# Retention turned in token halves through other buffers, stores on ScalarE's queue, dense weights fetched ahead

## The chip, the cores and the metric

The kernel runs on one core of a Trainium2 chip. The metric is the device time of one execution in microseconds (us). The core's engines are TensorE (PE: matmuls and transposes), VectorE (DVE), ScalarE (ACT), GpSimd (POOL) and SyncE (SP), which here issues every DMA. Each engine works through its own instructions in order.

## The reference

One block of 1024 tokens and 1024 channels, all in float32: differential attention beside chunkwise retention, merged by gates, then an MLP and a gated embedding.

```python
h = rms_norm(x, g_mix[i]);  proj = h @ w_in[i]
qa, ka, va, qr, kr, vr, gr, gate_a, gate_r = jnp.split(proj, split_idx, axis=-1)
# differential attention, 8 heads: softmax(q1 k1) - lam * softmax(q2 k2), times v, with ALiBi
# retention, 4 heads, chunks of 128, decay g per head:
def step(R, inp):
    qi, ki, vi = inp
    s = jnp.einsum('bnhk,bmhk->bhnm', qi, ki) * decay_intra
    intra = jnp.einsum('bhnm,bmhv->bnhv', s, vi)
    cross = jnp.einsum('bnhk,bhkv->bnhv', qi, R) * q_decay[None, :, :, None]
    R_new = R * chunk_decay[None, :, None, None] + jnp.einsum('bmhk,bmhv,hm->bhkv', ki, vi, k_decay)
    return R_new, intra + cross
yr = jax.nn.silu(gr) * rms_norm(retention(qr, kr, vr), g_ret_sub[i]).reshape(B, S, RET_V_W)
mixed = (jax.nn.sigmoid(gate_a) * (ya @ w_branch_diff[i]) + jax.nn.sigmoid(gate_r) * (yr @ w_branch_ret[i]))
x = x + mixed @ w_out[i];  x = x + square(relu(rms_norm(x, g_mlp[i]) @ w_ff1[i])) @ w_ff2[i]
x = x + sigmoid(rms_norm(x, g_ple[i]) @ w_ple_gate[i]) * (p[i] @ w_ple[i])
return rms_norm(x, g_final)
```

## The kernel before

TensorE multiplies float32 as pairs: `split` (L119 to L122) makes a high half by a cast on ACT (L121) and the rest by a subtraction on DVE (L122), and each product is three matmuls (hi hi, lo hi, hi lo). The stages follow one another: the in-projection to about 508 us; retention, four heads, to about 647 us; attention, eight heads, to about 1043 us; then the merge, the MLP and the rest.

**Dense steps as filler.** The gates' projections and later the branches' are written as generators in `queue`; one step is six 128x512 matmuls (L185 to L187), four steps fill a bank, sixteen do a unit of 256 columns for two token halves. `fill(n)` (L212) puts n steps between the pieces of retention (`RET_FILL`) and attention (`PLAN`). `cols_steps` loads and splits a unit's weights in its first step. A finished bank ("mm", two of them) is drained by `gate_out` (L444: activation L446, store of `gt_d` L447) or, in attention, by `fin_r`: the gate comes back by a load (L985), DVE multiplies it in (L989), and the product is stored (L990).

**Retention.** For each head `ret_qk` loads q and k (L701, 1 MB), multiplies the decays in (L705) and splits; `ret_sg` loads the silu gate (L733, 1 MB) into the slots S2 and S6 by turns; `ret_kn` transposes k (L721); `ret_scores` computes the masked scores in 24 matmuls (L749), writes them to the slot S8 (L751) and splits them to S7; `ret_chain` runs over eight chunks: the state's update (L766) goes to the back of S8 (L769, L771) and is split into `Gb`; the chunk's output is matmuls of S7 and `Gb` (L784), copied to S9 (L787 squares, L788 copies); after the last chunk POOL makes one power of 128x8 and DVE scales all chunks (L792). `ret_turn` turns the head over, for each of two channel blocks e and both token halves: four transposes (L802), the gate (L805, into "o" or "sq"), the split (high half to `Gb`), and two stores to `yr_d` (L88). 

**What sets the order.** A list scheduler puts each engine's instructions in a fixed order when the program is built. DMAs are tracked by eight semaphores by turns, so that each also waits for the one eight before it. A slot that is written again waits for every reader of its old content, stores included.

## Time and profile before

| | us |
|---|---|
| median of 3 runs | 1954.53 (1953.75 to 1958.95) |
| the profiled execution | 1956.08 |
| its span | 1954.1 |
| PE busy | 1898.3 (97%) |
| DVE busy | 1316.5 (67%) |
| ACT busy | 873.2 (45%) |

The span is the profiled execution without what lies around it (2.0 us). Matmuls overlap in the records, so that a dense 128x512 matmul is listed at 0.39 us while the next begins 0.23 us behind it; busy time says only where PE was not idle. The chain of waits gives PE 76% of the span, DVE 10% and DMA 6%.

### The profile page before, as it was taken

What the parts mean: (1) busy time and instruction counts of PE and PEld (TensorE: products, weight loads), DVE (VectorE), ACT (ScalarE), POOL (GpSimd) and SP (SyncE); (2) the same over time, 40 slices, a digit from 0 to 9 for tenths busy, and PEclk for the clock granted to TensorE, in tenths of its full rate; (3) what the DMA queues carried; (4) which work ended last, traced back from release to release, by engine and by line L of the source; (5) the groups of instructions that cost most, each with busy time, mean ns of one, the idle gap of its engine ahead of it and who ended that gap; (6) DMA issues with size and microseconds to landing.
All of it is one profiled execution on the core that took longest, in us unless ns stands there. A gap on an engine that the chain in (4) does not pass through costs nothing.

```text
span 1954.1 us, 24125 instructions
## 1 busy us (share of the span) xinstructions
PE 1898.3 (97%) x8976; PEld 1568.2 (80%) x8976; DVE 1316.5 (67%) x2047; ACT 873.2 (45%) x1370; POOL 108.5 (6%) x120
## 2 busy tenths in 40 slices
PE   8999999999999999999999998999999999999998
PEld 6888788888878778877788887788888888888886
DVE  5877765544667588888897436876766676776633
ACT  6533443334534477766675223433333443344522
POOL 1200000000000111111110002000000000000000
PEclk9999999999999999999999999999999999999999
DMA  8554554532777855876546323444546986555202
GB/s 276 180 173 164 174 179 164 180 120 98 270 256 223 219 155 137 253 221 180 161 154 197 124 76 97 140 148 149 164 132 206 374 313 226 196 183 186 94 11 76
DMA packets 238325, 343.36 MB, mean 176 GB/s; under 512 B 15104, under 2 KB 128896, under 8 KB 236928
## 3 DMA queue, kind: packets, MB, share of 16 engines
q1 hardware_dynamic: 238208, 341.83, 54.0%
q8 instruction: 70, 1.15, 0.2%
q14 instruction: 47, 0.39, 0.1%
HBM read 235.35 MB, written 106.43 MB: 175 GB/s over the span
## 4 chain that ended last, share of the span: by engine, by line
PE 76%; DVE 10%; DMA 6%; issue 4%; ACT 3%; POOL 2%; SPq 0%; POOLq 0%; DVEq 0%; ACTq 0%
PE mm L302 17%; PE qk L302 13%; PE qk L1279 6%; PE mm L187 4%; PE mm L185 4%; PE mm L186 4%; PE sm L1279 3%; PE mm L1279 3%; PE qk L853 2%; PE po L1279 2%; PE po L895 2%; PE qk L310 2%; DMA S<-in_w_in 2%; PE mm L199 1%; PE mm L200 1%
## 5 line engine op out<-in xcount | busy, mean ns | idle before, releaser
L185 PE MATMUL mm<-T,wh 128*128 128x512 f32 x352 | 140.2, 399 | 0.0
L186 PE MATMUL mm<-T,wh 128*128 128x512 f32 x352 | 139.9, 397 | 0.0
L187 PE MATMUL mm<-T,wl 128*128 128x512 f32 x352 | 139.3, 396 | 0.0
L860 ACT ACTIVATE S<-S,stat 128x256 f32<-128x256 f32 (+7 forms) x128 | 98.9, 775 | 37.3 <-DVE stat L855 36.9
L121 ACT CAST wh<-S 128x1024 fp32r<-128x1024 f32 (+1 forms) x60 | 69.2, 1167 | 94.0 <-issue 33.6
L853 PE MATMUL qk<-S,S 128*128 128x512 f32 (+3 forms) x384 | 103.2, 366 | 4.1 <-DVE stat L855 3.9
L229 POOL TENSOR_TENSOR stat<-stat,mhalf 128x1 f32<-128x1 f32 (+1 forms) x28 | 22.7, 809 | 1352.2 <-DVE stat L227 1352.2
L302 PE MATMUL mm<-S,T 128*128 128x512 f32 x384 | 94.3, 395 | 2.6 <-DVE S L122 1.9
L302 PE MATMUL mm<-T,raw 128*128 128x512 f32 x384 | 92.4, 389 | 2.9 <-DVE s L314 2.9
L302 PE MATMUL mm<-S,wh 128*128 128x512 f32 x384 | 93.1, 391 | 0.0
L302 PE MATMUL qk<-S,wh 128*128 128x512 f32 x384 | 92.2, 389 | 0.0
L302 PEld LDWEIGHTS mm<-S,T 128*128 128x128 f32 x384 | 73.0, 191 | 19.1 <-DVE S L122 2.3
L302 PEld LDWEIGHTS mm<-T,raw 128*128 128x128 f32 x384 | 72.0, 188 | 18.3 <-DVE s L314 3.3
L122 DVE TENSOR_TENSOR T<-T,T 128x1024 fp32r<-128x1024 f32 (+2 forms) x28 | 40.3, 1449 | 66.2 <-ACT T L121 66.2
L302 PEld LDWEIGHTS mm<-S,wh 128*128 128x128 f32 x384 | 72.5, 189 | 15.0
L302 PEld LDWEIGHTS qk<-S,wh 128*128 128x128 f32 x384 | 72.1, 188 | 15.0
L855 DVE CUSTOM_DVE_ANT_0 S<-qk,Gb 128x512 f32<-128x512 f32 (+3 forms) x128 | 72.6, 582 | 9.2 <-DMA Gb<-in_alibi 7.7
L121 ACT CAST S<-sm 128x512 fp32r<-128x512 f32 (+2 forms) x116 | 54.5, 493 | 49.4 <-PE sm L880 30.6
L853 PEld LDWEIGHTS qk<-S,S 128*128 128x128 f32 x384 | 62.6, 192 | 16.9 <-DVE stat L855 11.5
L187 PEld LDWEIGHTS mm<-T,wl 128*128 128x128 f32 x352 | 66.6, 189 | 11.7
L185 PEld LDWEIGHTS mm<-T,wh 128*128 128x128 f32 x352 | 66.7, 190 | 11.2
L186 PEld LDWEIGHTS mm<-T,wh 128*128 128x128 f32 x352 | 66.5, 189 | 11.0
(361 smaller groups left out, 4791.8 us busy)
## 6 DMA issues: line engine op xcount, KB each, us to landing
S<-in_w_in SPq DMA_DIRECT2D x52, 512.0 KB, 5.1
S<-qk_d SPq DMA_DIRECT2D x96, 256.0 KB, 5.8
S<-in_w_ff SPq DMA_DIRECT2D x40, 512.0 KB, 5.8
qk_d<-T SPq DMA_DIRECT2D x32, 512.0 KB, 5.1
...
```

Of the source, the lines that this page charges most:

```text
L121: nc.scalar.copy(out=hi, in_=src)
L122: nc.vector.tensor_tensor(out=lo, in0=src, in1=hi.bitcast(F32), op=ALU.subtract)
L185: nc.tensor.matmul(out=ps, lhsT=wh(kt), rhs=ah, start=(kt == 0), stop=False)
L186: nc.tensor.matmul(out=ps, lhsT=wh(kt), rhs=al, start=False, stop=False)
L187: nc.tensor.matmul(out=ps, lhsT=wl(kt), rhs=ah, start=False, stop=(kt == KT - 1))
L302: nc.tensor.matmul(out=ps, lhsT=x[:, k, :], rhs=y[:, k, :], start=(first and k == 0 and n == 0), stop=(k == 3 and n == 2), skip_group_chec ...
L310: nc.tensor.matmul(out=ps, lhsT=x[:, k, cs], rhs=y[:, k, :], start=(first and k == 0 and n == 0), stop=(k == 3 and n == 2), skip_group_che ...
L853: nc.tensor.matmul(out=ps, lhsT=qs[:, c, qsl], rhs=kk[:, c, k0:k0 + kw], start=(m == 0), stop=(m == 1))
L855: nc.vector.tensor_tensor_reduce(out=pr[:, c, k0:k0 + kw], in0=ps, in1=bias[0][:, S - w + k0:S - w + k0 + kw], scale=-1.0, scalar=mx[:, 2 ...
L860: nc.scalar.activation(out=pc, in_=pc, func=AF.Exp, scale=-1.0, bias=mx[:, 2 * c + n:2 * c + n + 1], accum_out=z[:, c:c + 1])
L895: nc.tensor.matmul(out=out, lhsT=v[:, k, :], rhs=a[:, k, q0:256], start=(k == 0 and n == 0), stop=(k == nkt - 1 and n == 2))
L1279: nc.tensor.matmul(out=ps, lhsT=a[x][:, m, k, st * P:(st + 1) * P], rhs=b[y][:, m, k, :], start=(g == 0 and k == 0 and n == 0), stop=(g == ...
```

## The change

- `gate_out`'s store goes on ScalarE's queue, and so do the stores of the high halves in `ret_turn`: 48 issues leave SP for ACT.
- `ret_turn` works on one token half at a time, both channel blocks in it, with three dense steps between the halves. Half 0 has its high halves in the front of S8 and f in "o" and "sq"; half 1 has its high halves in `Gb` and f in the back of S8.
- The power and the scaling of chunks 0 to 3 come after chunk 4, those of 4 to 7 at the end.
- The next head's decays stand after chunks 2 and 5, kept in program order.
- A class `Work` holds a dense unit: the next unit's weights are fetched when six steps of the present one are left and split when three are left. (The merge's first unit gets its weights by the same class.)

```diff
-    def move(out, in_):
-        nc.sync.dma_start(out=out.bitcast(F32), in_=in_.bitcast(F32))
+    def move(out, in_, eng=None):
+        (eng or nc.sync).dma_start(out=out.bitcast(F32), in_=in_.bitcast(F32))
...
+    def fetch_cols(w, c0):
+        raws = []
+        for k0 in (0, 4):
+            raws.append(raw_tile())
+            nc.sync.dma_start(out=raws[-1].rearrange("p (a n) -> p a n", n=256), in_=w_block(w, c0, 256, k0, k0 + 4))
+        return raws
+    def split_cols(raws):
+        hi, lo = slot("wh", F32R, bufs=2), slot("wl", F32R, bufs=2)
+        for i, raw in enumerate(raws):
+            split(raw, hi[:, i * 1024:(i + 1) * 1024], lo[:, i * 1024:(i + 1) * 1024])
+        return [a.rearrange("p (kt n) -> p kt n", n=256) for a in (hi, lo)]
...
+    class Work:
+        def __init__(self, steps, total, w=None, c0=0):
+            self.steps, self.left, self.w, self.c0 = steps, total, w, c0
+            self.raws = self.ops = None
+        def ready(self, to_split=True):
+            if self.w is None:
+                return
+            if self.raws is None:
+                self.raws = fetch_cols(self.w, self.c0)
+            if to_split and self.ops is None:
+                self.ops = split_cols(self.raws)
...
     def fill(n):
         while n > 0 and queue:
+            work = queue[0]
+            work.ready()
             try:
-                next(queue[0])
-                n -= 1
+                next(work.steps)
             except StopIteration:
                 queue.pop(0)
+                continue
+            n -= 1
+            work.left -= 1
+            if len(queue) > 1 and work.left in (6, 3):
+                queue[1].ready(work.left == 3)
...
-        nc.sync.dma_start(out=gt_d[:, unit, hs(half)], in_=o)
+        nc.scalar.dma_start(out=gt_d[:, unit, hs(half)], in_=o)
...
+        def decay(a):
+            x = tmp[:, a].rearrange("p (c n) -> p c n", n=P)
+            tc.keep_in_program_order(nc.vector.tensor_tensor(
+                out=x, in0=x, in1=rtab[h // 2][:, h % 2, a, :][:, None, :].broadcast_to([P, ST, P]), op=ALU.mult))
+        def parts(a):
             d = slot(("S0", "S1")[a], F32R).rearrange("p (a s) -> p a s", a=2)
             for half in range(2):
                 split(tmp[:, a, hs(half)], d[:, 0, hs(half)], d[:, 1, hs(half)])
...
+        decay(1)
+        kd = parts(1)
+        yield
+        decay(0)
+        yield
+        yield parts(0), kd
...
+        def norm(half):
+            four = slice(half * 4, half * 4 + 4)
+            r = rstd_of(ss[:, four], DV)
+            for c in range(half * 4, half * 4 + 4):
+                nc.vector.tensor_scalar(out=yn[:, c, :], in0=yn[:, c, :], scalar1=r[:, c % 4:c % 4 + 1],
+                                        scalar2=None, op0=ALU.mult)
...
-            fill(RET_FILL[0])
-        r = rstd_of(ss, DV)
-        for c in range(ST):
-            nc.vector.tensor_scalar(out=yn[:, c, :], in0=yn[:, c, :], scalar1=r[:, c:c + 1], scalar2=None, op0=ALU.mult)
+            fill_gates(RET_FILL[0])
+            if c == 4:
+                norm(0)
+            if c in (2, 5):
+                next(beside)
+        norm(1)
         return yn
-    def ret_turn(h, yn, sg):
+    def ret_turn(h, yn, sg, s8, half):
+        his = s8[:, 0:S] if half == 0 else slot("Gb", F32, (P, 1024))
         for e in range(2):
-            his = slot("Gb", F32R, (P, 1024)).rearrange("p (a s) -> p a s", a=2)
-            for half in range(2):
-                pt = bank("sm")
...
-                f = slot(("o", "sq")[half], F32, (P, HALF))
...
+            f = s8[:, S + e * HALF:S + (e + 1) * HALF] if half else slot(("o", "sq")[e], F32, (P, HALF))
...
+            hi = his[:, hs(e)].bitcast(F32R)
+            split(f, hi, f.bitcast(F32R))
+            move(yr_d[:, 0, h * 2 + e, hs(half)], hi, nc.scalar)
+            move(yr_d[:, 1, h * 2 + e, hs(half)], f.bitcast(F32R))
...
-        fill(RET_FILL[1])
-        ret_turn(h, yn, sg)
-    drain()
+        fill_gates(1)
+        ret_turn(h, yn, sg, s8, 0)
+        fill_gates(3)
+        ret_turn(h, yn, sg, s8, 1)
+    fill_gates(1 << 30)
```

`branch_work`, `last_gate` and `diff_half` are the old generators put into `Work`. Three places show what moves.

SP, at the change from head 0 to head 1; the loads are head 2's q and k and head 1's gate. Before:

```order
L88 DMA yr_d_72<-Gb_513_4005 128x512 [waits DMAHW7_49,Activation_49]
L88 DMA yr_d_72<-o_515_4011 128x512 [waits DMAHW0_49,DVE_49]
L701 DMA S2_522_4045<-qr_d_70 128x2048 [waits DMAHW1_49,DVE_49]
L88 DMA yr_d_72<-Gb_513_4005 128x512 [waits DMAHW2_49,Activation_49]
L88 DMA yr_d_72<-sq_517_4022 128x512 [waits DMAHW3_49,DVE_49]
L733 DMA S6_523_4047<-sg_d_71 128x2048 [waits DMAHW4_49,PE_49]
```

Now:

```order
L88 DMA yr_d_72<-o_511_3973 128x512 [waits DMAHW0_49,DVE_49]
L88 DMA yr_d_72<-sq_513_3984 128x512 [waits DMAHW2_49,DVE_49]
L149 DMA raw_638_4875<-in_w_in 128x4x256 [waits DMAHW4_49,DMAHW1_49,Activation_49]
L88 DMA yr_d_72<-S8_477_3714 128x512 [waits DMAHW6_49,DVE_49]
L736 DMA S2_525_4056<-qr_d_70 128x2048 [waits DMAHW7_49]
L88 DMA yr_d_72<-S8_477_3714 128x512 [waits DMAHW1_49,DVE_49]
L775 DMA S6_526_4058<-sg_d_71 128x2048 [waits DMAHW2_49,DMAHW3_49,PE_49,Activation_49]
```

Both f stores of half 1 now leave from S8; the second stands behind the 1 MB load.

DVE, at the change from head 1 to head 2, up to the write of the scores (L751 before, L793 now). Before:

```order
L122 TENSOR_TENSOR o_565_4351<-o_565_4351,Gb_563_4345 128x512 [waits Activation_49]
L805 SCALAR_TENSOR_TENSOR sq_567_4362<-sm_566_4357,gret_83,S6_523_4047 128x512 [waits DMAHW6_49,PE_49]
L122 TENSOR_TENSOR S3_568_4368<-sm_569_4369,S3_568_4368 128x512 [waits Activation_49]
L122 TENSOR_TENSOR sq_567_4362<-sq_567_4362,Gb_563_4345 128x512 [waits Activation_49]
L122 TENSOR_TENSOR S3_568_4368<-sm_570_4376,S3_568_4368 128x512 [waits Activation_49]
L751 TENSOR_TENSOR S8_574_4388<-sm_575_4389,s2_521_4043 128x512 [waits PE_49]
L122 TENSOR_TENSOR S7_573_4387<-S8_574_4388,S7_573_4387 128x512 [waits Activation_49]
L705 TENSOR_TENSOR S6_571_4383<-S6_571_4383,s2_521_4043 128x1024 [waits DMAHW2_49]
L751 TENSOR_TENSOR S8_574_4388<-sm_576_4405,s2_521_4043 128x512 [waits PE_49]
```

Now:

```order
L855 SCALAR_TENSOR_TENSOR S8_528_4061<-sm_566_4354,gret_83,S6_526_4058 128x512 [waits PE_49]
L122 TENSOR_TENSOR sq_560_4321<-sq_560_4321,S8_528_4061 128x512 [waits Activation_49]
L855 SCALAR_TENSOR_TENSOR S8_528_4061<-sm_567_4364,gret_83,S6_526_4058 128x512 [waits PE_49]
L122 TENSOR_TENSOR S8_528_4061<-S8_528_4061,Gb_565_4353 128x512 [waits Activation_49]
L122 TENSOR_TENSOR S3_568_4374<-sm_569_4375,S3_568_4374 128x512 [waits Activation_49]
L122 TENSOR_TENSOR S8_528_4061<-S8_528_4061,Gb_565_4353 128x512 [waits Activation_49]
L122 TENSOR_TENSOR S3_568_4374<-sm_570_4382,S3_568_4374 128x512 [waits Activation_49]
L740 TENSOR_TENSOR S6_571_4389<-S6_571_4389,s2_524_4054 128x1024 [waits DMAHW0_49]
L793 TENSOR_TENSOR S8_574_4394<-sm_575_4395,s2_524_4054 128x512 [waits DMAHW2_49,DMAHW3_49,DMAHW1_49,DMAHW4_49,DVE_49,PE_49]
```

The write of the scores now comes behind the decay (L740) and waits for four DMA semaphores beside PE.

PE in attention, at a branch unit of `w_branch_ret` (L185 to L187 before, L196 to L198 now). Before:

```order
L186 MATMUL mm_1135_7203<-T7_1087_6998,wh_1088_7003 128x512
L187 MATMUL mm_1135_7203<-T6_1086_6997,wl_1089_7004 128x512
L185 MATMUL mm_1135_7203<-T6_1086_6997,wh_1088_7003 128x512
L186 MATMUL mm_1135_7203<-T7_1087_6998,wh_1088_7003 128x512
L187 MATMUL mm_1135_7203<-T6_1086_6997,wl_1089_7004 128x512
L895 MATMUL po_1115_7115<-S8_1094_7027,S5_998_6593 128x256 [waits DVE_49]
L895 MATMUL po_1115_7115<-S7_1093_7026,S5_998_6593 128x256 [waits DMAHW5_49]
L895 MATMUL po_1115_7115<-S7_1093_7026,S5_998_6593 128x128
L895 MATMUL po_1115_7115<-S8_1094_7027,S5_998_6593 128x128
L895 MATMUL po_1115_7115<-S7_1093_7026,S5_998_6593 128x128
```

Now:

```order
L904 MATMUL qk_1133_7218<-S2_992_6583,S1_991_6582 128x256 [waits DVE_49]
L904 MATMUL qk_1133_7218<-S4_993_6584,S1_991_6582 128x256
L198 MATMUL mm_1131_7207<-T4_1084_7009,wl_1061_6888 128x512
L196 MATMUL mm_1131_7207<-T4_1084_7009,wh_1060_6887 128x512
L197 MATMUL mm_1131_7207<-T5_1085_7010,wh_1060_6887 128x512
L198 MATMUL mm_1131_7207<-T4_1084_7009,wl_1061_6888 128x512
L904 MATMUL qk_1148_7282<-S2_992_6583,S1_991_6582 128x512 [waits DVE_49]
L904 MATMUL qk_1148_7282<-S4_993_6584,S1_991_6582 128x512
L931 MATMUL sm_1142_7258<-ident_78,S3_1118_7149 128x128 [waits DVE_49,PE_49]
L931 MATMUL sm_1142_7258<-ident_78,S3_1118_7149 128x128 x3
L931 MATMUL sm_1143_7265<-ident_78,S3_1118_7149 128x128 [waits PE_49]
```

Before, the third bank of the unit is filled in one run, and 58 instructions of attention follow up to the fourth; now the third bank's matmuls stand among attention's.

## Rows read from the trace of the kernel before

**Rows 1.** The page: the busy time, share of the span and instructions of each engine.

```profile
PE 1898.3 (97%) x8976; PEld 1568.2 (80%) x8976; DVE 1316.5 (67%) x2047; ACT 873.2 (45%) x1370; POOL 108.5 (6%) x120
```

**Rows 2.** The view of waits, PE alone, 500 to 660 us (the four retention heads): engine, tile and line of the instruction that waited, whom it waited for, us in total, times, the longest in us.

```profile
PE qk L784 <- ACT Gb L121: 4.3, 2, 3.4
PE sm L802 <- DVE S L792: 2.1, 2, 1.4
PE sm L766 <- DVE S L751: 1.5, 1, 1.5
PE sm L802 <- DVE o L805: 0.8, 1, 0.8
PE sm L749 <- DVE S L122: 0.3, 1, 0.3
```

**Rows 3.** The view by windows: the stretch, its us, then busy us and count on PE, weight loads, DVE, ACT and POOL, the granted TensorE clock, the DMA share, GB/s. The change from head 0 to 1, from 1 to 2, and two stretches at half clock.

```profile
545.00:580.00 35.00, 31.36 (x172) 26.70 (x171) 23.73 (x49) 15.15 (x38) 1.65 (x1) 0.90 0.64 224
580.00:615.00 35.00, 31.16 (x187) 26.57 (x187) 26.22 (x54) 16.14 (x40) 2.05 (x1) 1.00 0.67 219
...
559.50:566.30 6.80, 5.27 (x22) 5.08 (x23) 3.32 (x10) 2.71 (x9) 0.00 (x0) 0.50 0.55 207
644.80:648.20 3.40, 3.29 (x15) 3.10 (x15) 3.40 (x6) 1.72 (x3) 0.00 (x0) 0.50 0.41 155
```

**Rows 4.** The timeline of PE at the change from head 0 to 1 and from 1 to 2: start and length in us, line, operation, tiles, shape, count, and in brackets the idle time before and what ended it.

```profile
551.96 2.89 PE L749 MATMUL sm<-S,S 128*128 128x128 f32 x24
...
561.03 0.58 PE L784 MATMUL qk<-Gb,S 128*128 128x256 f32 x1 [3.41 <-ACT Gb L121]
...
595.03 0.98 PE L766 MATMUL sm<-S,S 128*128 128x256 f32 x6 [1.52 <-DVE S L751]
```

**Rows 5.** The timeline of DVE there (columns as in Rows 4).

```profile
550.31 0.74 DVE L805 SCALAR_TENSOR_TENSOR sq<-sm,gret,S 128x512 f32<-128x512 f32 x1
...
551.74 0.69 DVE L122 TENSOR_TENSOR sq<-sq,Gb 128x512 fp32r<-128x512 f32 x1
...
553.44 0.69 DVE L751 TENSOR_TENSOR S<-sm,s 128x512 f32<-128x512 f32 x1 [0.21 <-PE sm L749]
...
593.15 1.23 DVE L705 TENSOR_TENSOR S<-S,s 128x1024 f32<-128x1024 f32 x1 [0.67 <-DMA S<-qr_d]
```

**Rows 6.** The timeline of ACT at the change from head 0 to 1 (columns as in Rows 4).

```profile
560.57 0.71 ACT L121 CAST Gb<-S 128x256 fp32r<-128x256 f32 x2 [3.60 <-DMA yr_d<-Gb]
```

**Rows 7.** The timeline of SP's DMA queue at the three changes of head: when each load or store was issued, and how long the issue held SP.

```profile
551.09 0.32 SPq L701 DMA_DIRECT2D S<-qr_d  x1
551.74 0.32 SPq L88 DMA_DIRECT2D yr_d<-Gb  x1
...
587.36 0.32 SPq L701 DMA_DIRECT2D S<-qr_d  x1
587.97 0.32 SPq L88 DMA_DIRECT2D yr_d<-Gb  x1
588.76 0.32 SPq L88 DMA_DIRECT2D yr_d<-sq  x1
...
625.95 0.32 SPq L88 DMA_DIRECT2D yr_d<-sq  x1
626.36 0.40 SPq L733 DMA_DIRECT2D S<-sg_d  x1
```

**Rows 8.** The view of DMA issues in narrow stretches around those same issues, in their order: tiles, count, KB, us from issue to landing.

```profile
S<-qr_d SPq DMA_DIRECT2D x1, 1024.0 KB, 8.7
...
yr_d<-Gb SPq DMA_DIRECT2D x1, 256.0 KB, 8.7
...
S<-qr_d SPq DMA_DIRECT2D x1, 1024.0 KB, 5.8
...
yr_d<-Gb SPq DMA_DIRECT2D x1, 256.0 KB, 6.0
...
yr_d<-sq SPq DMA_DIRECT2D x1, 256.0 KB, 5.7
...
S<-sg_d SPq DMA_DIRECT2D x1, 1024.0 KB, 5.1
yr_d<-sq SPq DMA_DIRECT2D x1, 256.0 KB, 2.3
```

**Rows 9.** The view by windows (columns as in Rows 3) in attention: a stretch without dense matmuls, the stretch behind it, and the part of the first at half clock.

```profile
853.00:871.00 18.00, 14.02 (x66) 10.10 (x65) 15.30 (x42) 12.70 (x23) 2.64 (x3) 0.91 0.87 235
871.00:900.00 29.00, 27.47 (x156) 23.07 (x155) 24.47 (x55) 17.89 (x37) 4.77 (x5) 1.00 0.73 190
866.70:870.10 3.40, 3.21 (x11) 2.75 (x12) 3.25 (x10) 3.16 (x5) 0.00 (x0) 0.50 0.69 219
```

**Rows 10.** The timeline of PE in the first of these stretches: the last dense matmul ahead of the gap and the first behind it.

```profile
853.57 0.39 PE L187 MATMUL mm<-T,wl 128*128 128x512 f32 x1
...
870.46 0.40 PE L185 MATMUL mm<-T,wh 128*128 128x512 f32 x1
```

**Rows 11.** The timeline of SP's queue and of DVE in it: the two loads of stored gates, and the first drain of a dense bank behind them.

```profile
858.59 4.26 SPq L985 DMA_DIRECT2D Ga<-gt_d  x2
...
868.57 0.69 DVE L989 TENSOR_TENSOR Ga<-mm,Ga 128x512 f32<-128x512 f32 x1
```

**Rows 12.** The view of waits of SP's own DMA queue, 500 to 900 us (columns as in Rows 2).

```profile
SPq L447 <- ACT Ga L446: 42.4, 14, 10.1
```

More of the change, by code (lines that the diff above doesn't have):

```diff
@@ L538, in block_kernel @@
         next(g)
-        queue.append(g)
+        queue.append(Work(g, 0))
     p1a = wide("S2")
@@ L674, in block_kernel, with cols_work, steps, gate_work @@
     hT = [[a11, a12], [a21, a22]]
-    def cols_steps(act, w, c0, evac, halves=(0, 1)):
-        wh, wl = load_cols(w, c0)
-        for half in halves:
-            for u in range(2):
-                yield from t_steps(act, half, lambda kt: wh[:, kt, u * P:(u + 1) * P],
-                                   lambda kt: wl[:, kt, u * P:(u + 1) * P], lambda ps: evac(u, half, ps))
-    def gate_steps(g, func, halves=(0, 1)):
-        return cols_steps(hT, w_in, C_GA + g * 256, lambda u, half, ps: gate_out(2 * g + u, half, func, ps), halves)
+    def cols_work(act, w, c0, evac, halves=(0, 1)):
+        def steps():
+            wh, wl = work.ops
+            for half in halves:
+                for u in range(2):
+                    yield from t_steps(act, half, lambda kt: wh[:, kt, u * P:(u + 1) * P],
+                                       lambda kt: wl[:, kt, u * P:(u + 1) * P], lambda ps: evac(u, half, ps))
+        work = Work(steps(), 8 * len(halves), w, c0)
+        return work
+    def gate_work(g, func, halves=(0, 1)):
+        return cols_work(hT, w_in, C_GA + g * 256, lambda u, half, ps: gate_out(2 * g + u, half, func, ps), halves)
     def bc4(a):
@@ L939, in block_kernel, with fill_gates @@
     for g in (4, 5, 6, 7):
-        queue.append(gate_steps(g, AF.Sigmoid, (1,) if g < 6 else (0, 1)))
-    gates = iter((0, 1, 2, 3))
+        queue.append(gate_work(g, AF.Sigmoid, (1,) if g < 6 else (0, 1)))
+    for g in range(3):
+        queue.append(gate_work(g, AF.Copy))
+    left = [48]
+    def fill_gates(n):
+        n = min(n, left[0])
+        left[0] -= n
+        fill(n)
     qk = ret_qk(0)
@@ L944, in block_kernel @@
     v = ret_v(0)
+    next(qk)
+    next(qk)
     qd, kd = next(qk)
@@ L947, in block_kernel @@
         if h == 0:
-            fill(2)
+            fill_gates(2)
         kn = ret_kn(tmp)
+        qk = iter((None, None))
         if h + 1 < HR:
@@ L974, in reload, with branch_work @@
             split(raw, *[a[:, k % 4:k % 4 + n, :] for a in act[half][k // 4]])
-    def branch_steps(act, w, g, finish, load):
+    def branch_work(act, w, g, finish, load):
         def evac(u, half, ps):
@@ L1000, in last_gate, with steps @@
     def last_gate(g):
-        for n, _ in enumerate(gate_steps(g, AF.Copy)):
-            yield
-            if n % 8 == 7:
-                reload_yr(n // 8)
+        work = gate_work(g, AF.Copy)
+        inner = work.steps
+        def steps():
+            for n, _ in enumerate(inner):
+                yield
+                if n % 8 == 7:
+                    reload_yr(n // 8)
+        work.steps = steps()
+        return work
     ya, mixed = [], []
@@ L1065, in block_kernel @@
                 reload(ya_d, ya, 0)
-                held[0] = load_cols(t["w_branch_diff"][0], 0)
                 for g in range(2):
-                    queue.append(diff_half(g, 0))
+                    early_diff[g] = Work(diff_half(g, 0), 8, t["w_branch_diff"][0], g * 256)
+                    queue.append(early_diff[g])
+                early_diff[0].ready()
             if (h, i) == (HA - 1, 7):
```

47 lines of the change are left out of this document (17 added, 30 removed).

## The prediction

> **What bounds the kernel now.** Read first the page: PE is busy 1898.3 us, 97% of the span [rows 1]. So DVE and ACT count only where PE waits for them, and the whole change can win no more than PE's idle time and its half-clock time in the stages that it touches. Second, the waits of PE in retention [rows 2] name the idle time: 4.3 us for the cast into `Gb`, 2.1 for the scaled chunks, 1.5 for the scores, 0.8 and 0.3 for the turn and the split of k, 9.0 in all. Third, the windows there [rows 3]: two stretches stand at half of the granted clock, 6.8 us with 5.27 busy and 3.4 us with 3.29 busy. Work done at half clock would take half at full, so they cost 5.27/2 + 3.29/2 = 2.6 + 1.6 = 4.2 us. Retention thus has about 13.2 us to give. Fourth, attention: between 853 and 871 us PE is busy 14.02 of 18 us, and 3.21 of that at half clock, a loss of 3.98 + 1.6 = 5.6 us; the 29 us behind it lose 1.53, which would be 0.95 in 18 us [rows 9]. The stretch thus gives 4.6 us more than its neighbour. In it no dense matmul runs from 853.57 to 870.46 [rows 10], since both dense banks are full: the drain by L989 comes at 868.57, behind a load of the gate that SP issues at 858.59 [rows 11].
>
> **What the change removes.** (1) The `Gb` wait. The longest wait of all, 3.41 us at 561.03 [rows 4], is ACT's cast, which itself waited 3.60 us for the store yr_d<-Gb [rows 6]: the state of the next head goes into the slot whose last stores are still under way. Now only one token half's high halves lie in `Gb`, on ACT's queue, and the chain starts later than that; I count all 4.3 us as gone. (2) The wait for the scores, 1.5 us: the second L751 stood in DVE's order behind the decay L705, which waited for the load of qr_d [rows 5]. The decays leave that place, or stand ahead of the first write, where another wait covers them. 1.5 gone. (3) The waits ahead of the turn: 2.1 + 0.8 + 0.3. Half of the chunks are now scaled during the chain, the other half while 18 dense matmuls at 0.23 us, 4.1 us, run between the half turns; the longest such wait was 1.4 [rows 2]. Gone, 3.2. (4) The two half-clock stretches of retention follow such waits; 4.2 gone with them. Sum in retention: 4.3 + 1.5 + 3.2 + 4.2 = 13.2 us.
> (5) In attention the third bank of the branch unit is now filled among attention's instructions and not ahead of them, so the waits from 853 to 871 have dense work beside them. 4.6 us gone; bounds 0 and 5.6.
> (6) SP's queue waited 42.4 us for ACT to finish gates [rows 12], and does so no longer. I count nothing for it: no row of PE's waits leads to a load that was late for that.
>
> **What it adds.** (7) The slot S8. Half 1 has its f in S8, and the next head's scores are written to S8. So L793 waits until the last f store has landed; behind it on DVE stands the whole next chain, and PE's first update L766 waits for it, since the scores hold the two "sm" banks until they are written. Before, L751 waited for PE alone [rows 5]. The price hangs on how long a store takes. Stores issued just behind a 1 MB load took as long as the load: 8.7 us behind the load of 551.09, 6.0 and 5.7 behind that of 587.36; one issued ahead of such a load took 2.3 [rows 7, 8]. The new order puts the last store behind a 1 MB load at each of the three changes of head: qr_d from 0 to 1 and from 1 to 2, sg_d from 2 to 3.
> The Trainium skill, page "DMA: Bandwidth & Descriptors", section "Queues, rings and completion order", says that a queue's descriptors are taken in ring order on each DMA engine, and that the engines take turns between the queues of different issuers. This trace agrees for the one queue that it has (5.7 to 8.7 us against 2.3). By that rule the high halves, on ACT's queue, escape the load while the f stores do not, which speaks against this part of the change; no run here shows two queues, and my sum is the same with the rule or without it.
> How much of a store's landing is covered: from the end of the last f subtraction (551.74 + 0.69 = 552.43) to the end of the 24 score matmuls (551.96 + 2.9, less the overlap, 554.6) are 2.2 us [rows 4, 5]; then come the dense matmuls that the new order has between the scores and L766, five, two and seven: 1.1, 0.45 and 1.6 us. Behind the landing come L793, 0.69, and about 0.25 until its reader starts, 0.95. The stall is landing + 0.95 - 2.2 - dense. From 0 to 1 the store is issued 1.4 us behind its load, as the one of 588.76 was: 5.7 gives 3.4 us, 8.7 gives 6.4, and I take the middle, 4.9, since the older load stood at that very change. From 1 to 2 the load goes out some 2.1 us ahead of the store (it waits only for the last L855), so 7.1 - 2.1 = 5.0 gives 3.2, and about 8.0 gives 6.3; on DVE the decay L740 also stands ahead of L793 and waits for the load, 5.8 + 1.23 = 7.0 behind its issue, the same moment. I take 3.3. From 2 to 3 the load is sg_d, 5.1 [rows 8], and the store, issued 1.4 behind it, lands some 0.9 after it, 4.6 from its own issue: 1.8; with 8.7, 5.9. I take 1.8. Sum 10.0, between 8.4 and 18.6; and 0 if the stores land in 2.3.
> (8) The clock behind these stalls. The wait of 3.41 us was followed by 6.8 us at half clock, worth 2.6; that of 1.52 by none: the stretch 580 to 615 is granted 1.00 [rows 3, 4]. Two of the new stalls are as long as the former. I take one and a half times 2.6, 3.9; bounds 0 and 7.8.
> (9) The transposes of k, which have two "sm" banks in common with the turn. They come directly behind half 1's turn: L855 twice (0.74 each, as L805), two casts and three subtractions of 0.69 stand on DVE and ACT before the scores can start, 3.65 us, against 2.8 us of matmuls beside them. About 0.9 at each of three changes: 2.6; bounds 0 and 4.2 (three times the longest old turn wait, 1.4 [rows 2]).
> (10) 48 more issues on ACT, which is busy 45% [rows 1]: nothing, except in a rival. Eight powers of four columns for four of eight, and later fewer dense matmuls behind the last turn: nothing that PE waits for.
>
> **The sum.** -13.2 - 4.6 + 10.0 + 3.9 + 2.6 = -1.3 us. The profiled execution took 1956.08, so 1954.8; the median of the runs lies 1.55 below it: 1953.2. I forecast **1953 us**. About 0.3%, 5.9 us, is what a measurement of this kernel can tell from no change; this is within it.
>
> **The rivals.** *The stores land fast.* With 2.3 us (terms 7 and 8 fall away) the sum is -13.2 - 4.6 + 2.6 = -15.2: 1939. For it: half of the stores have left SP's queue, so less stands ahead of the f stores, and a late load would let the store go first, as at 625.95. Against it: four stores beside a 1 MB load, and none below 5.7.
> *The S8 wait is larger than what it replaces.* All three landings at 8.7 and the clock halved each time: 18.6 + 7.8 + 2.6 - 13.2 - 4.6 = +11.2: 1966. It decides where the landings pass about 7 us each; then stalls and clock outweigh 15.2. For it: the 8.7 rows, and at the first change of head two loads of weights and the next v stand in SP's queue too. Against it: the rows of 6.0 and 5.7.
> *The dense part does nothing.* The fourth bank still waits for L1054 behind Ga<-gt_d, which stands in SP's order where it stood; if the third bank's matmuls merely shift the gap, term 5 is 0: +3.3, 1958. For it: the gate's load does not move. Against it: the longest stretch without dense work in PE's order falls from 58 instructions to about 30.
> *ACT is held by its own issues.* An issue on ACT waits for the DMA eight before it, which may be a 1 MB load, and ACT's casts for the chain stand behind it. One such wait of 5.7 us in each of two heads, less about 2 hidden, with the sum above: +6 or so, 1960. Against it: in the order the eighth DMA before lies tens of instructions back at most of these stores.
>
> **How the numbers follow.** Forecast 0.40 (of this 0.32 within 0.3%, 0.06 faster, 0.02 slower); fast stores 0.28, all faster; large S8 wait 0.17, slower by more than 0.3% except 0.01; the dense part does nothing 0.08, within; ACT held 0.07, slower but for 0.02. The last two lie between others in time. Faster 0.34, within 0.3% 0.43, slower 0.23. The range runs from the fast stores to the large S8 wait, as both hold more than 0.1: 1938 to 1966. The forecast's own range, from its bounds in terms 5, 7 and 9, is 1947 to 1959.
>
> **What would show it.** In the new trace: no wait of the chunk matmuls (L784, now L833) for the cast into `Gb` and none above 1 us at the turn; PE idle ahead of the first update (L766, now L815) of heads 1, 2 and 3, with DVE's L793 released by a DMA yr_d<-S; half clock behind at least one of them; f stores of S8 landing in 4.5 to 7 us and the ACT queue's high halves in less; 853 to 871 at full clock. It would be wrong if PE did not wait at L793's reader, or if these waits passed 4 us in all three heads, or if ACT's rows showed it idle at a store.

## The result, and the profile after

The changed kernel takes 1965.32 us (median of 7 runs, 1963.26 to 1968.04) against 1954.99 for the kernel before on the same chip: ratio 1.0053, 95% interval 1.0041 to 1.0065. It is slower by half a per cent. The forecast was 1953, no difference; the time is that of the rival "the S8 wait is larger than what it replaces" (1966). The profiled execution took 1966.27 us (span 1964.5), 10.2 more than that of before.

First the view of waits of the changed kernel, PE alone, 500 to 670 us (columns as in [rows 2]):

```profile
PE sm L815 <- issue: 12.3, 2, 6.4
PE sm L815 <- ACT S L121: 4.7, 1, 4.7
PE qk L833 <- DVE S L837: 1.5, 4, 0.4
PE sm L815 <- DVE S L793: 1.2, 1, 1.2
PE sm L852 <- DVE sq L855: 0.7, 1, 0.7
```

The waits of [rows 2] have gone, the one for `Gb` among them. In their place PE waits for itself at one line, L815, the first update of a head's state: 12.3 + 4.7 us in heads 1, 2 and 3. "issue" and L121 name no culprit; the timeline of DVE does. Here it is from the last f subtraction (S<-S,Gb) to the next head's first write of scores (L793), at the three changes of head:

```profile
547.46 0.68 DVE L122 TENSOR_TENSOR S<-S,Gb 128x512 fp32r<-128x512 f32 x1
556.82 1.29 DVE L793 TENSOR_TENSOR S<-sm,s 128x512 f32<-128x512 f32 x2 [8.07 <-DMA yr_d<-S]
...
588.33 0.68 DVE L122 TENSOR_TENSOR S<-S,Gb 128x512 fp32r<-128x512 f32 x1
594.37 1.23 DVE L740 TENSOR_TENSOR S<-S,s 128x1024 f32<-128x1024 f32 x1 [4.76 <-DMA S<-qr_d]
596.19 1.29 DVE L793 TENSOR_TENSOR S<-sm,s 128x512 f32<-128x512 f32 x2 [0.60 <-DMA yr_d<-S]
...
625.63 0.69 DVE L122 TENSOR_TENSOR S<-S,Gb 128x512 fp32r<-128x512 f32 x1
635.80 0.69 DVE L793 TENSOR_TENSOR S<-sm,s 128x512 f32<-128x512 f32 x1 [8.88 <-DMA yr_d<-S]
```

All three writes are released by a store yr_d<-S. From the end of the subtraction to the start of the write it is 8.7, 7.2 and 9.5 us (556.82 - 547.46 - 0.68, and so on), 25.3 in all; below this is called the *store delay*. PE waits 5.91, 4.75 and 6.42 us for it: L815 starts 0.1 us behind the end of the first of these writes (556.82 + 0.69 = 557.51). From the timeline of PE:

```profile
557.61 0.98 PE L815 MATMUL sm<-S,S 128*128 128x256 f32 x3 [5.91 <-issue]
```

The windows (columns as in [rows 3]) of the two changes of head that are shown there, and of the changed kernel's stretches at half clock:

```profile
545.00:580.00 35.00, 28.76 (x164) 24.51 (x163) 21.13 (x43) 13.58 (x36) 1.01 (x1) 0.90 0.56 199
580.00:615.00 35.00, 29.10 (x167) 25.21 (x166) 24.87 (x54) 15.78 (x38) 2.32 (x2) 0.90 0.55 203
...
519.10:522.50 3.40, 3.37 (x14) 2.97 (x14) 3.10 (x6) 2.80 (x9) 0.00 (x0) 0.50 1.02 371
556.60:563.50 6.90, 5.89 (x22) 5.34 (x23) 5.85 (x9) 3.05 (x5) 0.00 (x0) 0.51 0.54 173
594.20:601.00 6.80, 4.01 (x17) 3.85 (x18) 4.86 (x8) 3.17 (x8) 0.00 (x0) 0.50 0.51 209
635.10:642.00 6.90, 5.40 (x20) 5.02 (x21) 4.72 (x10) 2.39 (x6) 0.00 (x0) 0.51 1.04 228
672.70:676.10 3.40, 3.40 (x10) 2.92 (x11) 0.98 (x7) 2.16 (x5) 0.45 (x1) 0.50 1.03 219
```

Each of the three waits has a stretch of 6.8 or 6.9 us at half clock with it, and two shorter ones stand elsewhere, in head 0 and where attention begins (0.50 granted is 1.2 GHz). By the reckoning of the prediction (half of the busy time) they cost 2.9 + 2.0 + 2.7 and 1.7 + 1.7, together 11.0 us; those of before cost 4.2. One more stands later in attention, as one did before:

```profile
857.00:860.40 3.40, 3.19 (x9) 2.51 (x10) 1.82 (x8) 2.59 (x5) 0.66 (x1) 0.50 0.92 229
```

**The account.** In retention the change takes away 9.0 us of waits and 4.2 of half clock, and puts in 17.1 (the three waits), 1.2 (L815 behind L793 in head 0), 2.2 (L833, L852) and 11.0 (half clock): -13.2 + 31.5 = +18.3. Left out is a wait of 2.33 us at L904, the first of attention, just beyond that view: it ends at 672.69, where the last of the short stretches begins. With it the sum is +20.6. The 1.2 at L815 in head 0 and the stretch behind it are not the store's: with `Work` alone (*dense_ahead_only* below) PE waits 1.79 us there too, and 6.8 us stand at half clock.

A second way of counting: take PE's work as the pitch of its matmuls at full clock (0.227 us for one of 512 columns, less for the narrower) and call what elapses beyond it lost. From the 489th to the 625th us of that work, which is retention and the very beginning of attention, 24.0 us were lost before and 42.0 are lost now; from the 625th to the 970th, the rest of attention, 40.6 before and 33.3 now. Together +10.7, near the 10.2 by which the two executions differ. In retention that is +18.0, so the two ways agree within 3 us. These two *losses* are given for each run below. They shift by up to about 1 us, in all kernels alike, with the pitch that is taken for the narrow matmuls; and they are those of the profiled execution, which lies up to 4.3 us from the median of its kernel.

The timeline of SP's queue at the change from head 0 to 1, and two views of DMA issues in narrow stretches around 546.30 (on ACT's queue) and 549.52 (on SP's):

```profile
544.74 0.41 SPq L149 DMA_DIRECT2D raw<-in_w_in  x1
547.01 0.32 SPq L88 DMA_DIRECT2D yr_d<-S  x1
547.63 0.82 SPq L736 DMA_DIRECT2D S<-qr_d  x1
549.52 0.32 SPq L88 DMA_DIRECT2D yr_d<-S  x1
```

```profile
yr_d<-Gb ACTq DMA_DIRECT2D x1, 256.0 KB, 5.4
...
yr_d<-S SPq DMA_DIRECT2D x1, 256.0 KB, 7.1
```

A load of weights (0.5 MB) and the load of q and k (1 MB) lie ahead of the last f store on SP. The high halves on their own queue don't get past them: 5.4 us for this one, 7.2 for the next, about as long as the f stores. The same view for the last f stores at the other two changes, issued at 589.04 and 626.63:

```profile
yr_d<-S SPq DMA_DIRECT2D x1, 256.0 KB, 6.9
...
yr_d<-S SPq DMA_DIRECT2D x1, 256.0 KB, 9.0
```

What moved while the store of 549.52 was under way (the view of DMA, 549.52 to 556.64: packets, MB, share of 16 engines; q1 is SP's queue, and q10, which carries 48 stores of 256 KB, ACT's):

```profile
q1 hardware_dynamic: 661, 2.48, 85.4%
q10 hardware_dynamic: 290, 0.53, 19.2%
```

At the other two changes it is 2.25 and 2.55 MB on SP's queue, 0.59 and 0.51 on ACT's. So of some 3 MB that move beside each of these stores, ACT's queue has a fifth; the rest is SP's own.

### The profile page after: what moved, and what is told of

Same layout as the page of the kernel before. It is cut to its first block, busy times and chain, and to the rows that moved or that the text cites. A ratio compares the mean times of both kernels' runs of the same rounds, so it can differ in the third digit from the quotient of the medians.

```text
span 1964.5 us, 24111 instructions
## 1 busy us (share of the span) xinstructions
PE 1900.2 (97%) x8976; PEld 1573.4 (80%) x8976; DVE 1314.8 (67%) x2051; ACT 874.1 (44%) x1370; POOL 110.4 (6%) x124
## 4 chain that ended last, share of the span: by engine, by line
PE 76%; DVE 9%; DMA 5%; issue 4%; ACT 3%; POOL 2%; SPq 0%; ACTq 0%; POOLq 0%; DVEq 0%
PE mm L333 17%; PE qk L333 12%; PE qk L1349 6%; PE mm L198 4%; PE mm L197 4%; PE mm L196 4%; PE sm L1349 3%; PE mm L1349 3%; PE qk L904 3%; PE qk L341 2%; PE po L1349 2%; PE po L946 2%; PE mm L210 1%; PE mm L212 1%; PE mm L211 1%
## 5 line engine op out<-in xcount | busy, mean ns | idle before, releaser
L196 PE MATMUL mm<-T,wh 128*128 128x512 f32 x352 | 142.3, 404 | 0.0
L198 PE MATMUL mm<-T,wl 128*128 128x512 f32 x352 | 140.6, 400 | 0.0
L121 ACT CAST wh<-S 128x1024 fp32r<-128x1024 f32 (+1 forms) x60 | 69.2, 1167 | 94.8 <-issue 33.6
L904 PE MATMUL qk<-S,S 128*128 128x512 f32 (+3 forms) x384 | 101.6, 362 | 5.5 <-DVE stat L906 5.4
L260 POOL TENSOR_TENSOR stat<-stat,mhalf 128x1 f32<-128x1 f32 (+1 forms) x32 | 24.5, 766 | 1364.3 <-DVE stat L258 1364.3
L333 PEld LDWEIGHTS mm<-T,raw 128*128 128x128 f32 x384 | 73.1, 191 | 17.8 <-DVE s L345 2.5
L122 DVE TENSOR_TENSOR T<-T,T 128x1024 fp32r<-128x1024 f32 (+2 forms) x28 | 40.3, 1449 | 65.4 <-ACT T L121 65.4
L904 PEld LDWEIGHTS qk<-S,S 128*128 128x128 f32 x384 | 62.7, 191 | 18.9 <-DVE stat L906 11.8
L198 PEld LDWEIGHTS mm<-T,wl 128*128 128x128 f32 x352 | 67.4, 192 | 12.1
L196 PEld LDWEIGHTS mm<-T,wh 128*128 128x128 f32 x352 | 67.7, 192 | 10.9 <-DVE Ga L1054 0.3
L916 POOL TENSOR_SCALAR S<-S,stat,neglam 128x128 f32<-128x128 f32 (+3 forms) x64 | 53.5, 837 | 326.1 <-DVE stat L914 267.0
```

The costliest lines, as they stand in the source:

```text
L121: nc.scalar.copy(out=hi, in_=src)
L122: nc.vector.tensor_tensor(out=lo, in0=src, in1=hi.bitcast(F32), op=ALU.subtract)
L196: nc.tensor.matmul(out=ps, lhsT=wh(kt), rhs=ah, start=(kt == 0), stop=False)
L198: nc.tensor.matmul(out=ps, lhsT=wl(kt), rhs=ah, start=False, stop=(kt == KT - 1))
L333: nc.tensor.matmul(out=ps, lhsT=x[:, k, :], rhs=y[:, k, :], start=(first and k == 0 and n == 0), stop=(k == 3 and n == 2), skip_group_chec ...
L904: nc.tensor.matmul(out=ps, lhsT=qs[:, c, qsl], rhs=kk[:, c, k0:k0 + kw], start=(m == 0), stop=(m == 1))
```

## The experiments

All ratios are to the kernel before, run beside each kernel, with 95% intervals. Store delays are read from the timeline of DVE as above.

**1. One part undone at a time.** *f_in_o_sq*: the f of both halves goes through "o" and "sq", so no store holds S8.

```diff
-            f = s8[:, S + e * HALF:S + (e + 1) * HALF] if half else slot(("o", "sq")[e], F32, (P, HALF))
+            f = slot(("o", "sq")[e], F32, (P, HALF))
```

> The changed kernel, but the f of half 1 lies in "o" and "sq" like that of half 0, so that no late store leaves from S8. Theory A (the waits for S8 are the slowdown: 17.1 us idle ahead of L815 and some 2.6 us of half clock behind each): those three waits go, and what comes instead is at most the cast into Gb, 2 to 3 us a head, as the stores from Gb landed 7 us after their issue in the changed kernel; 1944 to 1954. Theory B (the bunch of stores and loads costs the same whoever waits for it): the time stays within 4 us of 1965, with as much idle time at Gb or at the gate's write into "o".

Measured: 1964.36, ratio 1.0057 (1.0042 to 1.0072); losses 34.4 in retention, 38.8 in attention. L815 waits no longer for stores, but the same stores hold "o" and "sq" now, and the turn itself waits. The waits of PE, then of DVE, 500 to 670 us:

```profile
PE sm L763 <- DVE o L855: 4.5, 3, 1.9
PE qk L833 <- DVE S L122: 4.0, 2, 3.8
PE sm L815 <- DVE S L793: 2.1, 1, 2.1
```

```profile
DVE o L855 <- DMA yr_d<-o: 11.6, 4, 4.0
```

PE idles less in these lines than in the changed kernel, about 12 us against 20, but more of its work is at half clock: 12.9 us against 11.0 by the same reckoning, with 10.2 us on end from 553.3. The time is that of theory B. So the slot is not the cause by itself: in either place the next writer of f's slot waits for a late store.

*f_on_act_queue*: the f stores go on ACT's queue too, away from SP's loads.

```diff
-            move(yr_d[:, 1, h * 2 + e, hs(half)], f.bitcast(F32R))
+            move(yr_d[:, 1, h * 2 + e, hs(half)], f.bitcast(F32R), nc.scalar)
```

> The changed kernel, but the f stores go on ScalarE's queue too. Theory A1 (an f store is late because it stands behind a 1 MB load in SP's own queue): on the other queue it lands in 2.3 to 4 us, the waits ahead of L815 fall below 2 us each, 1944 to 1950. Theory A2 (it is late because the DMA engines are full there, whatever the queue): it lands in 6 to 8 us as now, the waits stay at 4 to 6 us unless more dense matmuls lie beside them, 1957 to 1967.

Measured: 1976.57, ratio 1.0127 (1.0107 to 1.0146); losses 42.9 and 38.9. The view of DMA issues, 545 to 560 us:

```profile
S<-qr_d SPq DMA_DIRECT2D x1, 1024.0 KB, 7.3
...
yr_d<-Gb ACTq DMA_DIRECT2D x2, 256.0 KB, 9.1
yr_d<-S ACTq DMA_DIRECT2D x2, 256.0 KB, 8.3
```

The time lies above both ranges that were recorded. With no load on their queue, the stores take longer than the 1 MB load beside them: here, a queue of their own is no way past the loads.

*loads_behind_stores*: the loads of q and k and of the silu gate are kept behind the last f store in SP's order.

```diff
-        nc.sync.dma_start(out=tmp, in_=qr_d[:, h])
+        tc.keep_in_program_order(nc.sync.dma_start(out=tmp, in_=qr_d[:, h]))
...
-        nc.sync.dma_start(out=sg, in_=sg_d[:, 2 * h:2 * h + 2, :])
+        tc.keep_in_program_order(nc.sync.dma_start(out=sg, in_=sg_d[:, 2 * h:2 * h + 2, :]))
```

> The changed kernel, but the loads of the next q and k and of the gate are issued behind the last f store of the head before, on SP's queue. Theory A1 (queue order): the last f store lands in 3 to 5 us, since only stores stand ahead of it; the waits ahead of L815 fall to 0 to 2 us each and half clock behind them mostly goes; 1944 to 1950. Theory A2 (traffic): 2 MB less are under way beside it, so it is faster as well, 4 to 6 us; 1948 to 1957. Theory B: within 4 us of 1965, since the loads are late for the decays instead.

Measured: 1963.76, ratio 1.0050 (1.0032 to 1.0068); losses 38.6 and 33.1. The store delays fall from 8.7, 7.2 and 9.5 to 6.5, 5.6 and 6.9, 6.4 us less, but the waits of L815 only from 18.2 to 14.6: this order has no dense matmuls between the scores and the update. The time is that of theory B, but not by its reason: L793 still waits for stores (5.89 us at the first change). And the loads that were not pinned still lie ahead; from SP's timeline:

```profile
545.44 0.41 SPq L149 DMA_DIRECT2D raw<-in_w_in  x1
547.34 2.39 SPq L88 DMA_DIRECT2D yr_d<-S  x2
```

*decay_after_3*: the first decay after chunk 3.

```diff
-            if c in (2, 5):
+            if c in (3, 5):
```

> The changed kernel with the first decay after chunk 3 and not after chunk 2; all else as it is. Theory (the waits of S8 for the stores are the loss): the only gain is that the decay is no longer ahead of a wait for qr_d, L815 of head 0 (1.41 us and its half clock) and of head 2 keep or lose at most 1 to 2 us each: 1960 to 1966, with two or three waits of L815 above 4 us left. Rival (the place of the decays makes the waits, and is what made half1_in_s9 fast): 1950 or below, and at most one such wait left.

Measured: 1962.51, ratio 1.0042 (1.0030 to 1.0054); losses 34.3 and 34.0. The wait of head 0 goes; L815 still waits 12.8 us in three places, 4.8 at the longest. The decay's place is worth 0.11%, within the intervals, and is not the loss (the profiled execution, to which the losses belong, is 3.9 us faster than the median).

**2. Which stores belong on which queue.** Three runs complete a square with the changed kernel. *all_on_sp* has both of these lines, *halves_on_sp* the first, *gates_on_sp* the second:

```diff
-            move(yr_d[:, 0, h * 2 + e, hs(half)], hi, nc.scalar)
+            move(yr_d[:, 0, h * 2 + e, hs(half)], hi)
...
-        nc.scalar.dma_start(out=gt_d[:, unit, hs(half)], in_=o)
+        nc.sync.dma_start(out=gt_d[:, unit, hs(half)], in_=o)
```

> The changed kernel with every store on SP's queue as before; turn, slots, decays and Work stay changed. Theory A2 (the DMA engines are full at the change of head): landings stay at 5 to 9 us, 1962 to 1969. If the second queue made the f stores late: landings of 3 to 5 us, 1953 to 1960.

> The changed kernel with the high halves' stores back on SP's queue, the gates' stores still on ACT's: the other part of the same pair. Theory: one queue issues all eight stores of a head in order, the loads go out behind them, the last f stores land in 3 to 4.5 us and the waits of L815 sum to 5 to 9 us: 1946 to 1954. Rival (the gates' stores on ACT's queue are what hurts): 1960 or more.

> The changed kernel with the gates' stores back on SP's queue, the high halves' stores still on ACT's. Theory (it is the stores of the turn, split over two queues, that let SP get to the 1 MB loads ahead of the f stores): landings of the last f stores stay at 6 us or more in two or three of the heads, 1960 to 1966. Rival (SP must wait for ACT at the gates' stores, and that is what holds its 1 MB loads back): as all_on_sp, 1946 to 1952.

| high halves on | gates on | us | ratio | store delays, us | waits of L815, us | losses, us |
|---|---|---|---|---|---|---|
| ACT | ACT (the change) | 1965.32 | 1.0053 (1.0041 to 1.0065) | 8.7, 7.2, 9.5 | 18.2 | 42.0, 33.3 |
| ACT | SP | 1961.03 | 1.0036 (1.0025 to 1.0048) | 9.0, 7.5, 5.4 | 14.7 | 38.4, 32.2 |
| SP | ACT | 1950.47 | 0.9990 (0.9980 to 1.0001) | 5.3, 3.4, 3.8 | 8.9 | 27.7, 33.9 |
| SP | SP | 1948.37 | 0.9970 (0.9957 to 0.9984) | 4.4, 3.4, 4.1 | 6.7 | 24.2, 30.9 |

The high halves' queue is worth 0.63 to 0.66% (12 to 13 us), the gates' 0.17 to 0.20%, which is at the edge of what the intervals tell. From *halves_on_sp*, first the timeline of SP, then of DVE, at the change from head 0 to 1, and the DMA issue at 548.79:

```profile
546.01 0.32 SPq L88 DMA_DIRECT2D yr_d<-Gb  x1
546.74 0.32 SPq L88 DMA_DIRECT2D yr_d<-S  x1
547.34 0.32 SPq L88 DMA_DIRECT2D yr_d<-Gb  x1
548.79 0.32 SPq L88 DMA_DIRECT2D yr_d<-S  x1
549.16 0.42 SPq L736 DMA_DIRECT2D S<-qr_d  x1
...
554.93 0.43 SPq L149 DMA_DIRECT2D raw<-in_w_in  x1
```

```profile
547.30 0.68 DVE L122 TENSOR_TENSOR S<-S,Gb 128x512 fp32r<-128x512 f32 x1
553.23 1.29 DVE L793 TENSOR_TENSOR S<-sm,s 128x512 f32<-128x512 f32 x2 [4.64 <-DMA yr_d<-S]
```

```profile
yr_d<-S SPq DMA_DIRECT2D x1, 256.0 KB, 4.3
```

The f subtraction ends as in the changed kernel (547.98 against 548.14) and the store is issued 0.7 us sooner (548.79 against 549.52); what differs more is what lies ahead of it. In the order that the scheduler then makes, SP has all four stores first, then the load of q and k, and the load of weights that went out at 544.74 goes out at 554.93. The store lands in 4.3 us, not 7.1, and the score write starts 3.6 us earlier. The same holds at the other two changes: the last f store goes out just ahead of the 1 MB load and lands in 3.1 and 3.4 us. While these three stores are under way 1.55, 1.18 and 1.18 MB move, against 3.0, 2.8 and 3.1 in the changed kernel, at much the same rate (344 to 388 GB/s against 338 to 422). *all_on_sp* came out faster than either range recorded for it, with landings of 3.0 to 4.1 us as its second theory had them.

**3. The other parts alone.** *old_turn* is the changed kernel with the turn of before (`Gb` for the high halves, still on ACT's queue, "o" and "sq" for f, four dense steps ahead of it); *act_queue_only* is the kernel before with the two stores on ACT's queue; *dense_ahead_only* is the kernel before with `Work`.

> The changed kernel with the turn of before (channel block by channel block, high halves in Gb, f in "o" and "sq", four dense steps ahead of it); queue, decays, scaling in halves and class Work stay changed. If the half turns and their slots are the whole loss: 1950 to 1957. If ScalarE's queue or the decays cost as well: 1958 to 1965.

```diff
-        fill_gates(1)
-        ret_turn(h, yn, sg, s8, 0)
-        fill_gates(3)
-        ret_turn(h, yn, sg, s8, 1)
+        fill_gates(4)
+        ret_turn(h, yn, sg)
```

Measured: 1958.47, ratio 1.0019 (1.0005 to 1.0032); losses 24.5 and 40.3. Retention loses no more than before, so the changed kernel's loss there needs the half turns. The time lies at the foot of the range recorded for a queue or decays that cost as well; the profiled execution took 1954.15, 4.3 us less than the median, so its losses do not show what that cost is.

> The kernel before with the stores of gates and of the high halves on ScalarE's queue, nothing else. If the second queue neither gains nor costs: within 3 us of 1955. If a store there escapes SP's loads: the wait of 3.4 us at Gb goes with its half clock, 1947 to 1951. If ACT is held by its issues: 1958 or more.

```diff
-        nc.sync.dma_start(out=gt_d[:, unit, hs(half)], in_=o)
+        nc.scalar.dma_start(out=gt_d[:, unit, hs(half)], in_=o)
...
-                    move(yr_d[:, i, h * 2 + e, hs(half)], d)
+                    move(yr_d[:, i, h * 2 + e, hs(half)], d, nc.sync if i else nc.scalar)
```

Measured: 1959.70, ratio 1.0027 (1.0015 to 1.0040); losses 21.8 and 45.6. So the queue costs the old turn nothing in retention (24.0 before); what it loses lies in attention, 5.0 us more than before. Of this 3.3 are a stretch of 6.8 us at half clock from 998.4, which the kernel before does not have; what brings it about is open. The time falls in the range that was recorded for "ACT is held by its issues" (1958 or more), but its trace has no such hold: the longest issue on ACT takes 0.75 us. In the new turn the queue costs 0.83% (0.9970 against 1.0053, 16 us), 17.8 us by retention's loss (24.2 against 42.0): its price depends on who waits for the stores.

> The kernel before with the class Work alone (weights of the dense units fetched and split ahead); the turn, its buffers, queues and the decays are those of before. If attention's gain is that part's: 4 to 5.5 us faster than before, 1949.5 to 1951, with the stretch without dense matmuls at 853 us gone. If the gain came from where attention stood in time: within 2 us of 1955.

```diff
+            work = queue[0]
+            work.ready()
...
+            if len(queue) > 1 and work.left in (6, 3):
+                queue[1].ready(work.left == 3)
```

Measured: 1956.21, ratio 1.0010 (0.9999 to 1.0020); losses 22.4 and 40.6. The gap of [rows 10] is still there; the last dense matmul ahead of it and the first behind:

```profile
854.73 0.39 PE L198 MATMUL mm<-T,wl 128*128 128x512 f32 x1
871.45 0.40 PE L196 MATMUL mm<-T,wh 128*128 128x512 f32 x1
```

Fetching the weights ahead gains nothing by itself.

**4. Half 1 in S9.** *half1_in_s9* takes the stores of half 1 out of the way: once half 1 is transposed, S9 is free until the next head's first chunk output, long after the scores. Its high halves go to the front of S9, its f to the back; both transposes of a half stand ahead of its gates, since the gates overwrite S9, and the first decay is after chunk 3. ACT's queue stays. *half1_in_s9_on_sp* puts the stores back on SP besides.

```diff
-        his = s8[:, 0:S] if half == 0 else slot("Gb", F32, (P, 1024))
+        his = s8[:, 0:S] if half == 0 else yt[:, 0:S]
...
-            f = s8[:, S + e * HALF:S + (e + 1) * HALF] if half else slot(("o", "sq")[e], F32, (P, HALF))
+        for e, pt in enumerate(pts):
+            f = yt[:, S + e * HALF:S + (e + 1) * HALF] if half else slot(("o", "sq")[e], F32, (P, HALF))
```

> The changed kernel, but half 1 leaves S8 and Gb: its high halves go into the front of S9 and its f into the back (S9 is one tile for all heads, both transposes of a half come before the gates), and the first decay stands after chunk 3 instead of 2, so that DVE's order has no decay ahead of L793. Theory A (PE waits at the change of head for slots whose stores landed 4 to 9 us late, be it S8, "o" or Gb): S9's chunks are rewritten 4 us and more later, so those waits go and with them most of the half clock in retention: 1940 to 1949. Theory B (the bunch of stores and loads costs the same wherever it lies): 1960 to 1967, with as much waiting at S9.

> half1_in_s9 with both kinds of store back on SP's queue. Theory (the second queue only delays the stores' landings, and its price is paid by an engine that waits for a landing): with half 1 in S9 nothing near waits for a store, so the queue is worth little here, though it was worth 17 us with half 1 in S8: 1934 to 1942, and the f stores land in 3 to 5 us instead of 5 to 8. Rival (the second queue costs PE time by itself, by its issues on ACT or by its share of the DMA engines): some 10 us less than half1_in_s9, 1929 or below.

Measured: 1938.86, ratio 0.9915 (0.9890 to 0.9939), losses 15.1 and 32.3; and 1937.14, ratio 0.9914 (0.9901 to 0.9927), losses 16.2 and 32.2. Both beat both kernels, the first by 1 us more than its range. The waits of PE in *half1_in_s9*, 500 to 670 us, and below them DMA issues, 545 to 560:

```profile
PE sm L814 <- issue: 1.8, 1, 1.8
PE qk L832 <- DVE S L122: 0.8, 4, 0.2
PE qk L832 <- DVE S L836: 0.6, 1, 0.6
```

```profile
yr_d<-S SPq DMA_DIRECT2D x2, 256.0 KB, 6.5
...
yr_d<-S ACTq DMA_DIRECT2D x1, 256.0 KB, 7.1
```

The stores of half 1 are about as late as in the changed kernel, and PE waits for none of them. One wait behind a store is left: the high halves of half 0 still leave from S8, and L793 waits 2.88 us for one of them at the first change, PE 1.8 us behind it. Here the queue makes no difference that can be measured (0.9915 and 0.9914), though it is worth 16 us where S8 waits for half 1. The windows of *half1_in_s9_on_sp* at the changes of head stand at 34.54 and 33.72 busy of 35:

```profile
545.00:580.00 35.00, 34.54 (x213) 29.20 (x211) 27.84 (x58) 16.64 (x41) 2.38 (x2) 1.00 0.82 287
580.00:615.00 35.00, 33.72 (x195) 28.99 (x195) 28.08 (x57) 16.85 (x41) 2.32 (x2) 0.95 0.62 209
```

## Why the prediction was wrong

The mechanism was named, with its place; its sizes were wrong, and with them the choice between the forecast and a rival.

- **Terms 1 to 4 (what goes in retention), -13.2.** Right: of the waits of [rows 2] only one of 0.7 us at the turn is left (L852, counted under term 9), and the half clock behind them is gone.
- **Term 5 (attention), -4.6.** Right in size, in part by luck. From the 760th to the 820th us of PE's work, where the gap lay, 14.1 us were lost before and 9.5 are lost now: 4.6. But the stretch at half clock, which the term counted as gone, is still there (857.00 to 860.40); what went is idle time. The reason is not the fetching ahead, where 13.9 are lost with `Work` alone. The longest run of attention's matmuls and transposes without dense work in PE's trace is 58 before and with `Work` alone, 42 in *old_turn*, 38 in *act_queue_only* and 32 in the changed kernel. So it shortens when the queue alone is changed, without half turns; what decides it is not shown. Another 2.7 us are gained elsewhere in attention; from what is open. The rival "the dense part does nothing" falls for the whole change and holds for `Work`.
- **Term 6 (SP no longer waits for gates), 0.** No gain; if anything, moving these stores costs 0.17 to 0.20%.
- **Term 7 (the wait for S8), +10.0. This is the step that failed.** The formula held: landing + 0.95, less 2.2 for the scores, less the dense matmuls. The cover comes out at (25.3 + 3 x 0.95 - 17.1)/3 = 3.7 us a change, against 3.25 priced. What it covers did not hold: I took landings of 7.2, 5.0 and 4.6 us and counted them from the end of the last f subtraction; the store delays, which stand in their place, are 8.7, 7.2 and 9.5, and the waits 5.91, 4.75 and 6.42 against 4.9, 3.3 and 1.8. At the first change the landing itself, 7.1 us from issue, is as I took it; but the store was ready at 548.14 and issued at 549.52, and these 1.4 us I had put at nothing. At the other two the landings were mis-sized: 6.9 and 9.0 us from issue. I took them from stores of the kernel before [rows 8], counting only the one 1 MB load ahead of the store in the new order, and the high halves on ACT's queue at nothing. But a load of weights had moved ahead of the f stores as well (544.74, from 554.93 where one queue has all high halves), as the order printed with the change shows. From 1 to 2 the gate's load of 1 MB went out 1.6 us behind the store (590.65) and moved beside it. From 2 to 3 a load of attention's v stood ahead (623.17 in SP's timeline, 627.79 in *halves_on_sp*). The upper bound, 18.6, held.
- **Term 8 (the clock behind these waits), +3.9.** 7.6 us: a full stretch with each of the three waits, its upper bound of 7.8. Two short stretches that I did not price add 3.4.
- **Term 9 (the transposes of k), +2.6.** L763 does not wait. (The 3.65 us in it are 3.55 by the prices that it names, which changes nothing.) Some 2.2 us of other small waits (L833, L852) stand in its place.
- **Term 10 (48 issues on ACT), nothing.** As a cost of ACT's time, true. As a cost of the change, wrong: this is the part that decides its sign, since without it the change is faster (0.9970). I had looked at what the issues do to ACT, and not at what SP does with the room that they leave. The rival "ACT is held by its own issues" is not borne out: the longest issue on ACT takes 0.93 us in the changed kernel (at 543.58), and *half1_in_s9* has the same issues. The rival "the stores land fast" falls too: no store delay of the changed kernel is below 7.2.

With the sizes as measured, retention comes to -13.2 + 17.1 + 11.0 + 1.2 + 2.2 = +18.3 where I had +3.3, and the profiled execution to 1956.08 + 18.3 - 7.3 = 1967.1; it took 1966.27. With the wait at L904 it would be 2.3 more, so the sum is good to some 3 us and its closeness is partly luck. The same goes for the rival's 1966: its mechanism came true, but its stalls, clock and transposes were 29.0 us where 31.5 to 33.8 came, and its 4.6 in attention were 7.3. (Its 18.6 of stalls goes by a landing of about 8.0 and not 8.7 at the second change.)

Of the signs, PE's idle time at L815 of heads 1 to 3, the release of L793 by yr_d<-S and the half clock behind came as said. The last f stores did not land in 4.5 to 7 us but in 7.1, 6.9 and 9.0, and 853 to 871 was not at full clock. And one sign of being wrong came: the waits passed 4 us in all three heads.

The prediction weighed the Trainium skill, page "DMA: Bandwidth & Descriptors", section "Queues, rings and completion order", by which the DMA engines take turns between the queues of different issuers; from this it reasoned that the high halves would escape the load. The traces do not bear out the escape: 5.4 and 7.2 us on ACT's queue beside a load on SP's, and 8.3 to 9.1 where all stores of the turn are on it. The same section of the Trainium skill says that the increment of a completion lands only after every earlier write from that DMA engine, across its queues, which would let stores of both queues land late together as they do here; no run separates this from mere sharing. The section "Issuing engines are not separate DMA queues" of that page of the Trainium skill says that issuing from several engines only saves issue time. Here moving the stores changed more than that: the order of what the other engine issues, and with the half turns the time, by 16 us.

Open is how much of the store delay is order and how much is the sharing of the DMA engines by two queues. The bytes speak for the order: about 3 MB moved beside a late store and 1.2 to 1.6 beside one of *halves_on_sp*, and only 0.5 to 0.6 of the 3 went through ACT's queue. Pinning two loads took 6.4 us off the delays, one queue for all stores 13.4; no run pinned every load, so the split itself is not shown.
